# A two-layer decoder trunk in float32: six seven-product pairs per gate/up duo, ScalarE and VectorE in an order set by clocks, and some low parts made by DMA

## The chip, the cores and the metric

The kernel runs on one core of one Trainium2 chip. The metric is the device time of one execution in microseconds (us), lower is better. The profile and the times below are of the kernel before the change.

## The reference

Two layers over 256 tokens with a model width of 2048. The first mixes tokens by gated linear attention, the second by differential attention over shared keys and values; after each stands a gated feed-forward network (FFN). The change touches the two FFNs.

```python
D_MODEL, SEQ, D_FF = 2048, 256, 5632

def swiglu(h, w_gate_up, w_down):
    gate, up = jnp.split(h @ w_gate_up, 2, axis=-1)
    return (jax.nn.silu(gate) * up) @ w_down

for i in range(2):
    h = rmsnorm(x, pre_mix_g[i])
    mix = gla_mixer(h, ...) if i == 0 else diff_mixer(h, ...)
    x = x + rmsnorm(mix, post_mix_g[i])
    f = swiglu(rmsnorm(x, pre_ffn_g[i]), ffn_w_gate_up[i], ffn_w_down[i])
    x = x + rmsnorm(f, post_ffn_g[i])
```

Everything is float32. The weights of an FFN are a 2048 x 11264 matrix (gate and up) and a 5632 x 2048 matrix (down).

## The kernel before

**Three products for one.** A float32 operand is split into a high part of the type fp32r and a low part, the rest. A product is then three TensorE (PE) matmuls into one PSUM bank: high by high, high by low, low by high (`triple`, L442 to L444; for whole chunks L370 to L372). The tokens stand in two blocks of 128, and a matmul has 128 x 128 of tokens as the stationary side and 128 x 512 of weights as the moving one.

**The stream of weights.** `weight_stream` lists in the order of use every unit of weights that PE takes. A plain unit is a "raw" tile of 128 x 1024: two k-tiles of 128 rows by a chunk of 512 columns. `load` (L259) fetches it on SyncE's queue (SP) into one of five slots (NRAW). `split` casts it on ScalarE (ACT, L294) to `hi` and subtracts on VectorE (DVE, L296) to get `lo`. Pairs of hi and lo have nine slots (NRING). PE `take`s a unit, makes 12 matmuls (two k-tiles, two token blocks, three products) and `free`s it. At each take and free `pump` writes out the conversions for which there is room, and the loads for which a raw slot is done with.

**Duos and fast pairs.** A gate chunk c and the up chunk 11 + c go together as a duo (`gated_duo`, `duo_apart`). A duo has eight pairs of k-tiles s. A pair that isn't listed as fast is two plain units, 24 matmuls. For a fast pair seven products do the work of eight, as in Strassen's scheme: 21 matmuls. It has four kinds of unit. Its two raw tiles r1 and r2 go through four sums on DVE (`sums`, L317), which write over the raw tiles and into one tile `sum` of half the width. Then "a" is r1 itself, "b" and "c" are the summed r2 and r1, all 1024 wide, and "d" is the half tile, 512 wide. So three whole tiles and one half are cast and have their low parts made. The half goes to places in the tile `f_ffn_rest`. The seven products need seven PSUM banks; `acc` has six buffers, `tp` has two, which transposes use as well. FAST_FFN names the fast pairs: 0, 2, 3, 4 and 6 of eight. Chunk 1 has four (FAST_SECOND), and chunk 0 is done plainly (`gated_first`). There are ten duos in an FFN, twenty in all.

**The order of steps.** `ffn_steps` lists the up and down steps of an FFN: up 0, up 1, down of chunks 0 and 1, up 2, and so on. A down step has eight plain units (sixteen for a group of two chunks in two steps), 22 times eight in the two FFNs. After a duo, `early` and `late` put the banks together on DVE (L1126), ACT copies one bank (L1137) and applies silu (L1148), and DVE multiplies by the up part (L1130). `gate_T` transposes the result some ticks later (`defer`, `tick`; a tick is a unit or half of one). `evac` adds the down sums (L1202, L1200).

**What sets the order.** The tile scheduler orders the instructions of each engine by simulated times from the order in which the program writes them, with a conversion written as one piece: the cast and the subtraction together.

Of the kernel before, what the change touches and what calls it, by code (L numbers as in the profile page):

```python
# [11 lines left out]
F32 = mybir.dt.float32  # L12
# [3 lines left out]
ALU = mybir.AluOpType  # L16
# [24 lines left out]
FAST_FFN = (0, 2, 3, 4, 6)  # L41
# [6 lines left out]
NRAW, NRING = 5, 9  # L48
V_BEGIN, V_EVERY, V_Q = 16, 3, 1

# [29 lines left out]

def weight_stream():
# [9 lines left out]
    def duo(c1, c2, fast):  # L91
        for s in range(8):
            if s in fast:
                out.extend(("duo", (c1, c2, s), kind) for kind in ("a", "b", "c", "d"))
            else:
                out.extend((name, (n, s), "plain") for name, n in (c1, c2))
# [35 lines left out]
    ffn(1)  # L132
    return out
# [53 lines left out]
class Trunk:  # L187
    def __init__(self, ctx, tc, t):
# [16 lines left out]
        self.subs = {}  # L205
        self.raws = {}
        self.n_dma = self.n_conv = self.n_take = self.n_free = 0
        self.pool_lo = set()
        self.n_narrow = 0
# [46 lines left out]
    def load(self):  # L256
# [3 lines left out]
        self.raws[self.n_dma] = raw  # L260
        self.n_dma += 1
# [28 lines left out]
    def split(self, src, gp=False):  # L290
        nc = self.nc
        w = src.shape[-1]
        hi, lo = self.places(w)
        nc.scalar.copy(hi, src)  # L294
        eng = nc.gpsimd if gp else nc.vector
        eng.tensor_tensor(out=lo, in0=src, in1=hi.bitcast(F32), op=ALU.subtract)  # L296
        return hi, lo

# [11 lines left out]
    def sums(self):  # L310

        nc = self.nc
        r1, r2 = self.pending
        t2 = self.narrow[0].tile([P, C], F32, tag="sum", name=self.uid("sum"))

        def add(out, in0, in1):
            nc.vector.tensor_tensor(out=out, in0=in0, in1=in1, op=ALU.add)  # L317

        add(r1[:, :C], r1[:, :C], r2[:, :C])
        add(r2[:, :C], r2[:, :C], r2[:, C:])  # L320
        add(t2, r1[:, :C], r2[:, C:])
        add(r1[:, C:], t2, r1[:, C:])
        self.pending = r1, r2, t2

    def convert(self):
        n = self.n_conv
        kind = self.stream[n][2]
        self.n_done += kind in ("plain", "beside", "c", "b")
        if kind == "plain":
            self.subs[n] = self.split(self.raw(), n in self.pool_lo) if n else self.split_halves(self.raw())  # L330
        elif kind == "beside":
            self.subs[n] = self.split_beside(self.raw())
        elif kind == "a":
            self.pending = self.raw(), self.raw()
# [1249 lines left out]
```

## Time and profile before

| | |
|---|---|
| median of 3 runs | 2179.21 us (2178.58 to 2179.89) |
| span of the profiled execution | 2177.2 us |
| PE busy, share of the span | 2162.6 us, 99% |
| DVE busy | 1932.7 us, 89% |
| ACT busy | 1267.2 us, 58% |
| GpSimd (POOL) busy | 35.6 us, 2% |
| DMA engines' mean share, SP's queue | 60.2%, 436.44 MB |
| the FFNs | 372 to 1085 us and 1470 to 2177 us of the span |

A row of the timeline gives the start and length in us, the engine, the line, the operation, output and inputs, and in brackets what it waited for. A row of a group ends with its count, the busy time and the mean ns of one, and the idle time ahead of it with what ended it. PEclk in tenths is the clock that TensorE was granted; 9 is 90% or more. PE's matmuls overlap in the pipeline, so the distance of their starts is their price, not the length of one.

### The profile page before, as it was taken

How to read it: one execution, taken by the hardware profiler on the slowest of the kernel's cores; microseconds unless marked ns; L12 is line 12 of the kernel's file. 1: busy time of each engine (PE TensorE's matmuls, PEld its weight loads, DVE VectorE, ACT ScalarE, POOL GpSimd, SP SyncE). 2: the span in 40 equal slices, each digit the busy share in tenths (PEclk: the TensorE clock that was granted, in tenths of full speed). 3: DMA queues.
4: the chain of work that ended last, by engine and by line, in shares of the span. 5: the costliest groups of instructions: out<-in, count | busy, mean ns of one | idle time of the engine just before them, and what ended most of it. 6: DMA issues, size and time to landing. Idle time of an engine off the chain costs nothing.

```text
span 2177.2 us, 28399 instructions
## 1 busy us (share of the span) xinstructions
PE 2162.6 (99%) x10098; PEld 1798.1 (83%) x10098; DVE 1932.7 (89%) x2646; ACT 1267.2 (58%) x1744; POOL 35.6 (2%) x66
## 2 busy tenths in 40 slices
PE   9999999999999999999999999999999999999998
PEld 8887788888888888888878888888888888888886
DVE  7989988998999999998898567889999999999986
ACT  8656665665655555554676455556566555555553
POOL 1000000000000000000000000000000000000000
PEclk9999999999999999999999999999999999999999
DMA  8545566666655566665757655465656555666664
GB/s 309 169 149 191 177 228 213 213 221 215 228 176 199 194 213 213 194 224 189 243 187 248 186 174 161 151 235 189 231 194 223 182 185 195 209 206 212 212 213 135
DMA packets 123315, 440.09 MB, mean 202 GB/s; under 512 B 13899, under 2 KB 16628, under 8 KB 121380
## 3 DMA queue, kind: packets, MB, share of 16 engines
q1 hardware_dynamic: 121996, 436.44, 60.2%
q10 hardware_dynamic: 1176, 1.84, 0.3%
q8 instruction: 79, 1.29, 0.2%
q14 instruction: 64, 0.52, 0.1%
HBM read 429.82 MB, written 9.97 MB: 202 GB/s over the span
## 4 chain that ended last, share of the span: by engine, by line
PE 96%; DVE 2%; DMA 1%; issue 1%; ACT 1%; POOL 0%; SPq 0%; DVEq 0%; POOLq 0%; ACTq 0%
PE acc L444 13%; PE acc L443 13%; PE acc L442 13%; PE acc L372 10%; PE acc L370 10%; PE acc L371 10%; PE acc L585 8%; PE acc L586 4%; PE tp L443 3%; PE tp L444 3%; PE tp L442 3%; PE tp L606 1%; DVE lo L296 1%; PE acc L1307 0%; PE acc L1346 0%
## 5 line engine op out<-in xcount | busy, mean ns | idle before, releaser
L294 ACT CAST hi<-raw 128x1024 fp32r<-128x1024 f32 x905 | 929.5, 1051 | 656.6 <-DVE raw L317 272.7
L296 DVE TENSOR_TENSOR lo<-raw,hi 128x1024 fp32r<-128x1024 f32 x903 | 1077.6, 1220 | 151.8 <-ACT hi L294 148.9
L370 PE MATMUL acc<-hi,f_ffn_gT 128*128 128x512 f32 x704 | 274.1, 390 | 0.0
L371 PE MATMUL acc<-lo,f_ffn_gT 128*128 128x512 f32 x704 | 274.0, 390 | 0.0
L372 PE MATMUL acc<-hi,f_ffn_gT 128*128 128x512 f32 x704 | 268.9, 389 | 0.0
L444 PE MATMUL acc<-hi,h_ffn 128*128 128x512 f32 x666 | 259.6, 390 | 0.0
L443 PE MATMUL acc<-lo,h_ffn 128*128 128x512 f32 x666 | 259.2, 389 | 0.0
L442 PE MATMUL acc<-hi,h_ffn 128*128 128x512 f32 x666 | 258.4, 390 | 0.0
L372 PEld LDWEIGHTS acc<-hi,f_ffn_gT 128*128 128x128 f32 x704 | 132.2, 188 | 27.3
L370 PEld LDWEIGHTS acc<-hi,f_ffn_gT 128*128 128x128 f32 x704 | 132.2, 188 | 27.2
L371 PEld LDWEIGHTS acc<-lo,f_ffn_gT 128*128 128x128 f32 x704 | 132.2, 188 | 27.0
L444 PEld LDWEIGHTS acc<-hi,h_ffn 128*128 128x128 f32 x666 | 125.0, 188 | 26.5 <-issue 0.6
L443 PEld LDWEIGHTS acc<-lo,h_ffn 128*128 128x128 f32 x666 | 125.1, 188 | 25.9
L442 PEld LDWEIGHTS acc<-hi,h_ffn 128*128 128x128 f32 x666 | 125.0, 188 | 25.9
L585 PE MATMUL acc<-h_q,hi 128*128 128x512 f32 x256 | 92.5, 401 | 0.0
L585 PE MATMUL acc<-h_kv,hi 128*128 128x512 f32 x256 | 90.6, 399 | 0.0
L585 PE MATMUL acc<-h_mix,hi 128*128 128x512 f32 x256 | 90.5, 398 | 0.0
L317 DVE TENSOR_TENSOR raw<-sum,raw 128x512 f32<-128x512 f32 x122 | 84.2, 690 | 3.5
L317 DVE TENSOR_TENSOR raw<-raw 128x512 f32<-128x512 f32 x122 | 84.2, 690 | 3.3
L317 DVE TENSOR_TENSOR raw<-raw,raw 128x512 f32<-128x512 f32 x122 | 83.9, 687 | 2.0
L317 DVE TENSOR_TENSOR sum<-raw,raw 128x512 f32<-128x512 f32 x122 | 83.5, 684 | 0.0
L586 PE MATMUL acc<-h_q,lo 128*128 128x256 f32 x256 | 73.2, 286 | 0.0
(416 smaller groups left out, 3912.4 us busy)
## 6 DMA issues: line engine op xcount, KB each, us to landing
raw<-in_w_gu_dram SPq DMA_DIRECT2D x352, 512.0 KB, 4.4
raw<-in_w_d_dram SPq DMA_DIRECT2D x176, 512.0 KB, 5.2
raw<-in_gla_w_r_dram SPq DMA_DIRECT2D x32, 512.0 KB, 4.4
raw<-in_gla_w_v_dram SPq DMA_DIRECT2D x32, 512.0 KB, 4.0
raw<-in_gla_w_out_dram SPq DMA_DIRECT2D x32, 512.0 KB, 4.5
raw<-in_w_v_dram SPq DMA_DIRECT2D x32, 512.0 KB, 4.7
raw<-in_w_k_dram SPq DMA_DIRECT2D x32, 512.0 KB, 4.0
raw<-in_diff_w_q_dram SPq DMA_DIRECT2D x32, 512.0 KB, 3.5
```

The costliest lines, as they stand in the source:

```text
L294: nc.scalar.copy(hi, src)
L296: eng.tensor_tensor(out=lo, in0=src, in1=hi.bitcast(F32), op=ALU.subtract)
L317: nc.vector.tensor_tensor(out=out, in0=in0, in1=in1, op=ALU.add)
L370: nc.tensor.matmul(ps, ah, rh, start=(kt == 0), stop=False)
L371: nc.tensor.matmul(ps, ah, rl, start=False, stop=False)
L372: nc.tensor.matmul(ps, al, rh, start=False, stop=(kt == 2 * ns - 1))
L442: nc.tensor.matmul(ps, ah, wh, start=first, stop=False)
L443: nc.tensor.matmul(ps, ah, wl, start=False, stop=False)
L444: nc.tensor.matmul(ps, al, wh, start=False, stop=last)
L585: nc.tensor.matmul(ps, lh, aT.both(kt), start=(kt == 0), stop=False)
L586: nc.tensor.matmul(ps[:, SEQ:], ll, aT.hi(kt), start=False, stop=(kt == KT - 1))
L606: nc.tensor.transpose(tp[:, j, :], src[:, j * P : (j + 1) * P], self.ident)
```

## The change

**Sixth fast pair.** FAST_FFN gets pair 5. Chunk 1 keeps its four pairs, so 18 of the 20 duos have one pair more; the program has 54 matmuls fewer that are 512 wide (8686 before, 8632 now). In the FFNs the kinds come in the order a, d, b, c, and the first sum is now written to the half tile, not over r1. Banks 5 and 7 of a duo are the ones in `tp`, not 6 and 7. The half tile has two places in the ring `fp` and two in `f_ffn_rest`, before three in `f_ffn_rest`.

**Order by clocks.** A conversion is taken apart into a cast, the sums and the subtraction, each put with its inputs and a duration into a line for ACT or DVE (`sources`, `open`). The code keeps a clock for PE, ACT, DVE and SP: PE's goes on by 227 ns a matmul, and a line's next piece is written as soon as its start by these clocks isn't later than PE's (`emit`, `until`). From the second step of an FFN up to the one before the last (`by_clock`), ACT and DVE issue in the order written; the scheduler's order stands only elsewhere. Silu and the multiplication of a duo go through a side line that is served first.

**Low parts by DMA.** Of every eight down units the third, fifth and seventh (66 in all) have no subtraction on DVE. ACT writes minus the raw tile into the `lo` tile (L408), and a transfer that GpSimd issues adds the weights to it from HBM once more, this time in full float32 (L409). PE's matmul on `lo` waits for that transfer.

**Smaller moves.** `gate_T` of chunk 0 comes after 2 ticks, before 4; the set-up of the attention (`side`) is deferred by 5 ticks, before 20. With the new order its eight DVE steps (L914 to L938) stand in one lump in the first FFN, ahead of a low part.

```diff
-FAST_FFN = (0, 2, 3, 4, 6)
+FAST_FFN = (0, 2, 3, 4, 5, 6)
...
+LO_BY_DMA = {"w_d0": (2, 4, 6), "w_d1": (2, 4, 6)}
...
+LEFT = 1
+PASS_NS, TURN_NS, HELD_NS = 227, 109, 127
+LOAD_NS, LAND_NS, SUM_LAND_NS = 1600, 2800, 10000
...
+def dve_ns(n):
+    return 70 + 1.04 * n
...
+def act_ns(n):
+    return 90 + 0.84 * n
...
+def kinds(chunk):
+
+    return ("a", "d", "b", "c") if chunk[0].startswith("w_gu") else ("a", "b", "c", "d")
...
-    def split(self, src, gp=False):
-        nc = self.nc
-        w = src.shape[-1]
-        hi, lo = self.places(w)
-        nc.scalar.copy(hi, src)
-        eng = nc.gpsimd if gp else nc.vector
-        eng.tensor_tensor(out=lo, in0=src, in1=hi.bitcast(F32), op=ALU.subtract)
-        return hi, lo
...
+            if kind == "a":
+                add(0, raws, lambda: (third(), r1[:, :C], r2[:, :C]))
+                line = self.queue["dve"]
+                if len(line) > 1 and line[-2][1] == ("lo", n - 1) and self.stream[n - 1][2] == "c":
+                    line[-2], line[-1] = line[-1], line[-2]
+                return r1, raws[:1]
+            if kind == "d":
+                add(1, [t1], lambda: (r2[:, :C], r2[:, :C], r2[:, C:]))
+                add(2, [t1], lambda: (r1[:, :C], t[0], r2[:, C:]))
+                return t, [t1]
+            if kind == "b":
+                add(3, [t3], lambda: (r1[:, C:], r1[:, :C], r1[:, C:]))
+                return r2, [t2]
+            return r1, [t4]
...
+        def negated():
+            hl.extend(self.places(w))
+            nc.scalar.activation(hl[1], src(), AF.Copy, scale=-1.0)
+            nc.gpsimd.dma_start(hl[1], self.t[name][idx], accum_op=ALU.add)
+
+        def cast():
+            if not by_dma:
+                hl.extend(self.places(w))
+            nc.scalar.copy(hl[0], src())
+            self.n_done += by_dma
+
+        def rest():
+            eng.tensor_tensor(out=hl[1], in0=src(), in1=hl[0].bitcast(F32), op=ALU.subtract)
+            self.n_done += kind in ("plain", "c", "b")
...
+        if by_dma:
+            self.queue["act"].append((n, ("lo", n), after, act_ns(w), negated))
+            self.queue["act"].append((n, ("hi", n), after, act_ns(w), cast))
         else:
...
+            self.queue["act"].append((n, ("hi", n), after, act_ns(w), cast))
+            self.queue["dve"].append((n, ("lo", n), [("hi", n)], dve_ns(w), rest))
...
+        start = max([self.clock[eng]] + [self.ends[k] for k in after])
+        if start > now:
+            return False
+        line.popleft()
+        fn()
+        self.clock[eng] = self.freed = start + ns
+        self.ends[key] = start + ns + (SUM_LAND_NS if key[0] == "lo" and eng == "act" else 0)
...
+        with self.tc.manual_schedule(engines={mybir.EngineType.Activation, mybir.EngineType.DVE}):
+            yield
+            self.settle()
+            self.until(self.n_conv - 1)
...
-        self.narrow, self.n_narrow = (fp, 0, 3), 0
+        self.narrow, self.n_narrow = (fp, 2, 2), 0
...
-                    self.defer(20, side)
+                    self.defer(5, side)
...
+        step(0, *plan[0])
+        with self.by_clock():
+            for n in range(1, len(plan) - LEFT):
+                step(n, *plan[n])
+        for n in range(len(plan) - LEFT, len(plan)):
+            step(n, *plan[n])
```

How the order changes is seen in the fourth duo of the first FFN. First DVE at its last fast pair, pair 6, before the change. raw_5715 and raw_5763 are the pair's r1 and r2; the rows begin at its first sum (the row with raw_5715 and raw_5763 in, raw_5715 out) and go to its last low part.

```order
L317 TENSOR_TENSOR raw_5715<-raw_5715,raw_5763 128x512
L317 TENSOR_TENSOR raw_5763<-raw_5763 128x512
L317 TENSOR_TENSOR sum_5822<-raw_5715,raw_5763 128x512
L317 TENSOR_TENSOR raw_5715<-sum_5822,raw_5715 128x512
L296 TENSOR_TENSOR lo_5828<-raw_5763,hi_5827 128x1024
L296 TENSOR_TENSOR f_ffn_rest<-sum_5822,f_ffn_rest 128x512
L296 TENSOR_TENSOR lo_5837<-raw_5715,hi_5836 128x1024
```

The same pair on DVE after the change, with raw_5789 as r1 and raw_5834 as r2; lo_5886 belongs to pair 5.

```order
L341 TENSOR_TENSOR sum_5897<-raw_5789,raw_5834 128x512
L418 TENSOR_TENSOR lo_5886<-raw_5745,hi_5885 128x1024
L418 TENSOR_TENSOR lo_5895<-raw_5789,hi_5894 128x1024
L341 TENSOR_TENSOR raw_5834<-raw_5834 128x512
L341 TENSOR_TENSOR raw_5789<-sum_5897,raw_5834 128x512
L418 TENSOR_TENSOR lo_5903<-sum_5897,hi_5902 128x512
L341 TENSOR_TENSOR raw_5789<-raw_5789 128x512
L418 TENSOR_TENSOR lo_5923<-raw_5834,hi_5922 128x1024
L418 TENSOR_TENSOR lo_5938<-raw_5789,hi_5937 128x1024
```

The four sums stood in one row, each reading what the one before had written; now low parts stand between them.

Next DVE from the pair's last low part (lo_5837) to the end of the duo, the first operation of `early`, before the change. All rows but the last are low parts of plain units: two of pair 7, then down units.

```order
L296 TENSOR_TENSOR lo_5837<-raw_5715,hi_5836 128x1024
L296 TENSOR_TENSOR lo_5857<-raw_5775,hi_5856 128x1024
L296 TENSOR_TENSOR lo_5869<-raw_5792,hi_5868 128x1024
L296 TENSOR_TENSOR lo_5878<-raw_5804,hi_5877 128x1024
L296 TENSOR_TENSOR lo_5896<-raw_5831,hi_5895 128x1024
L296 TENSOR_TENSOR lo_5914<-raw_5840,hi_5913 128x1024
L296 TENSOR_TENSOR lo_5926<-raw_5860,hi_5925 128x1024
L296 TENSOR_TENSOR lo_5938<-raw_5872,hi_5937 128x1024
L1126 TENSOR_TENSOR hs_5965<-acc_5707,sg_5964 128x512
```

The same stretch of DVE after the change, from the pair's last low part (lo_5938) on.

```order
L418 TENSOR_TENSOR lo_5938<-raw_5789,hi_5937 128x1024
L418 TENSOR_TENSOR lo_5947<-raw_5851,hi_5946 128x1024
L418 TENSOR_TENSOR lo_5959<-raw_5889,hi_5958 128x1024
L418 TENSOR_TENSOR lo_5968<-raw_5906,hi_5967 128x1024
L418 TENSOR_TENSOR lo_5989<-raw_5941,hi_5988 128x1024
L1297 TENSOR_TENSOR hs_6005<-tp_5753,sg_6004 128x512
L1297 TENSOR_TENSOR sg_6004<-acc_5731,hs_6005 128x512
```

Seven low parts stood between the pair's last one and the first sum of the banks; now there are four, and DVE is less far ahead of PE when it turns to the banks.

Last ACT at the same place, around its copy of the bank (sg_5964), before the change.

```order
L294 CAST hi_5913<-raw_5840 128x1024
L294 CAST hi_5925<-raw_5860 128x1024
L1137 COPY sg_5964<-acc_5666 128x512
L294 CAST hi_5937<-raw_5872 128x1024
L294 CAST hi_5949<-raw_5881 128x1024
L294 CAST hi_5958<-raw_5899 128x1024
L294 CAST hi_5986<-raw_5917 128x1024
L1148 ACTIVATE sg_5964<-sg_5964,rs_ffn_0_3744 128x512
```

ACT around the same copy (sg_6004) after the change.

```order
L414 CAST hi_5967<-raw_5906 128x1024
L414 CAST hi_5988<-raw_5941 128x1024
L408 ACTIVATE lo_6001<-raw_5953 128x1024
L1303 COPY sg_6004<-acc_5712 128x512
L414 CAST hi_6000<-raw_5953 128x1024
L414 CAST hi_6028<-raw_5962 128x1024
L408 ACTIVATE lo_6036<-raw_5974 128x1024
L1317 ACTIVATE sg_6004<-sg_6004,rs_ffn_0_3744 128x512
L1317 ACTIVATE sg_6004<-sg_6004,rs_ffn_1_3849 128x512
L414 CAST hi_6035<-raw_5974 128x1024
```

The negated copies of the first two low parts by DMA of that down step (lo_6001 and lo_6036) stand on ACT among the casts and the bank's copy; GpSimd issues the transfer into each right after it. PE has 50 matmuls between the end of pair 6 and its first use of lo_6001. The raw tile of lo_6001 is loaded into the slot of raw_5851, which DVE is done with at lo_5947.

207 lines of the change are left out of this document (153 added, 54 removed).

## The prediction

> **What bounds the kernel now.** I read the head of the page first, then the busy time by stretch, then the matrix engine's timeline, and last the waits and groups of the engines that feed it. The head gives one core, 2177.2 us, with TensorE (PE) busy throughout at the full granted clock:
>
> ```profile
> span 2177.2 us, 28399 instructions
> PE 2162.6 (99%) x10098; PEld 1798.1 (83%) x10098; DVE 1932.7 (89%) x2646; ACT 1267.2 (58%) x1744; POOL 35.6 (2%) x66
> PEclk9999999999999999999999999999999999999999
> ```
>
> A busy PE need not be a PE at its pace, so the stretches of the two FFNs and, inside the first, one period of two duos with their sixteen down units come next (columns: us, then busy time and count per engine, clock, DMA share, GB/s):
>
> ```profile
> 372.00:1085.00 713.00, 712.76 (x3205) 589.99 (x3204) 656.96 (x826) 408.11 (x510) 3.12 (x5) 1.00 0.62 207
> 1470.00:2177.00 707.00, 697.87 (x3131) 577.79 (x3131) 645.04 (x810) 391.89 (x481) 3.12 (x5) 1.00 0.60 199
> 575.00:700.00 125.00, 125.00 (x562) 103.68 (x561) 118.58 (x141) 69.73 (x78) 0.00 (x0) 1.00 0.60 202
> ```
>
> In that period VectorE (DVE) is busy 118.58 of 125 us, ScalarE (ACT) 69.73 and PE all of it. The timeline of PE at the end of a duo (the fourth of the first FFN) gives the pace:
>
> ```profile
> 655.33 0.39 PE L442 MATMUL acc<-hi,f_ffn_rest 128*128 128x512 f32 x1
> 655.56 0.39 PE L443 MATMUL acc<-lo,f_ffn_rest 128*128 128x512 f32 x1
> ...
> 660.09 0.39 PE L442 MATMUL acc<-hi,h_ffn 128*128 128x512 f32 x1
> ```
>
> Left out are 19 rows of the same kind, so 21 steps take 4.76 us: 0.2267 us a matmul, without a gap. The check is the period: two duos of five fast pairs (21 matmuls each) and six plain units (12 each), with sixteen down units (12 each), are 546 matmuls, 123.8 us, and 16 transposes take the rest of 125. So in the FFNs the number of matmuls is the time, as long as the low parts come ahead of PE. DVE, which makes them, has only some 5% to spare.
>
> **The matmuls.** Eighteen of the twenty duos get a sixth fast pair (chunk 1 of each FFN keeps four). A fast pair is 21 matmuls where two plain units are 24. That removes 18 x 3 = 54 matmuls, 54 x 0.2267 = 12.2 us, all of it on the path. Nothing else leaves PE.
>
> **DVE's work.** The groups of the same period, 575 to 700 us, for DVE (xcount, then busy us and mean ns):
>
> ```profile
> L296 DVE TENSOR_TENSOR lo<-raw,hi 128x1024 fp32r<-128x1024 f32 x59 | 70.4, 1220 | 4.4 <-ACT hi L294 4.1
> L317 DVE TENSOR_TENSOR raw<-sum,raw 128x512 f32<-128x512 f32 x10 | 6.9, 691 | 0.3
> L296 DVE TENSOR_TENSOR f_ffn_rest<-sum,f_ffn_rest 128x512 fp32r<-128x512 f32 x10 | 6.8, 685 | 0.0
> ```
>
> A fast pair has four sums at 0.69, three whole low parts at 1.22 and one half at 0.69: against two plain units it adds 4 x 0.69 + 0.69 + 1.22 = 4.7 us. In the period that is two more pairs, +9.3 us. Six of its sixteen down units lose their DVE low part, -6 x 1.22 = -7.3 us. The new order sets low parts between sums that need each other, and what that is worth stands in DVE's timeline of the fourth duo's last fast pair (pair 6):
>
> ```profile
> 637.37 4.62 DVE L296 TENSOR_TENSOR lo<-raw,hi 128x1024 fp32r<-128x1024 f32 x4
> 642.03 0.69 DVE L317 TENSOR_TENSOR raw<-raw,raw 128x512 f32<-128x512 f32 x1
> 642.76 0.69 DVE L317 TENSOR_TENSOR raw<-raw 128x512 f32<-128x512 f32 x1
> 643.37 0.68 DVE L317 TENSOR_TENSOR sum<-raw,raw 128x512 f32<-128x512 f32 x1
> 644.09 0.69 DVE L317 TENSOR_TENSOR raw<-sum,raw 128x512 f32<-128x512 f32 x1
> 644.70 1.23 DVE L296 TENSOR_TENSOR lo<-raw,hi 128x1024 fp32r<-128x1024 f32 x1
> 645.85 0.69 DVE L296 TENSOR_TENSOR f_ffn_rest<-sum,f_ffn_rest 128x512 fp32r<-128x512 f32 x1
> 646.45 5.76 DVE L296 TENSOR_TENSOR lo<-raw,hi 128x1024 fp32r<-128x1024 f32 x5
> 653.23 2.48 DVE L296 TENSOR_TENSOR lo<-raw,hi 128x1024 fp32r<-128x1024 f32 x2 [1.02 <-ACT hi L294]
> 656.21 1.23 DVE L296 TENSOR_TENSOR lo<-raw,hi 128x1024 fp32r<-128x1024 f32 x1 [0.50 <-ACT hi L294]
> 657.57 0.69 DVE L1126 TENSOR_TENSOR hs<-acc,sg 128x512 f32<-128x512 f32 x1
> ```
>
> A step that waits for the one before starts 0.72 us after it, one that doesn't 0.61 us: two such waits a pair, 0.2 us. Twelve pairs make -2.4 us. DVE's period is then 118.6 + 9.3 - 7.3 - 2.4 = 118.2 us (120.6 without the last term), against PE's 125 - 1.4 = 123.6. On the average PE stays the bound, and DVE costs nothing.
>
> **The lead inside a duo.** Averages hide where it gets tight. By the program's order the third whole low part of pair 4 is the first of the four at 637.37, done at 638.6, and that of pair 6 the first of the five at 646.45, done at 647.7. PE reaches them here (the second is the row at 655.56 above):
>
> ```profile
> 645.36 0.39 PE L443 MATMUL acc<-lo,f_ffn_fast 128*128 128x512 f32 x1
> ```
>
> So DVE leads by 6.8 us at pair 4 and by 7.9 us at pair 6, the plain pair 5 between them having given time back. A whole low part takes 1.13 us in a row of them (5.76 less 1.22, over four). A fast pair costs DVE 4.42 + 2 x 1.13 = 6.7 us before, 6.5 after, against PE's 4.76. With pair 5 fast, pairs 5 and 6 take 2 x 1.74 from the lead of 6.8: 3.3 us is left at pair 6. The rows of the order give another reading: ahead of the first sum that needs pair 6's banks stand seven whole low parts before and four now. DVE's turn at that sum comes with the end of pair 6 on PE, so four at 1.13, less the last, which may just have begun, leave a lead of 2.3 us at least. I take 3; the lowest lead of a duo shrinks from 7 to 3 us, and no stall comes of it.
>
> **ACT and the DMA.** The negated copy is a second ACT pass of a 1024-wide tile, and a fast pair has three whole casts and one half where two stood:
>
> ```profile
> L294 ACT CAST hi<-raw 128x1024 fp32r<-128x1024 f32 x58 | 59.7, 1051 | 49.2 <-DVE raw L317 26.0 <-PE acc L444 6.8 <-DMA raw<-in_w_d_dram 5.8
> L294 ACT CAST f_ffn_rest<-sum 128x512 fp32r<-128x512 f32 x10 | 6.1, 614 | 3.3 <-DVE sum L317 3.3
> ```
>
> Per period: 69.7 + 6 x 1.05 + 2 x 1.67 = 79.4 us of 123.6. ACT has room. The transfers:
>
> ```profile
> q1 hardware_dynamic: 121996, 436.44, 60.2%
> raw<-in_w_gu_dram SPq DMA_DIRECT2D x352, 512.0 KB, 4.4
> raw<-in_w_d_dram SPq DMA_DIRECT2D x176, 512.0 KB, 5.2
> ```
>
> A packet takes 0.602 x 16 x 2177.2 / 121996 = 0.172 us, so a load of 128 packets holds the sixteen engines for 1.4 us. Six more in a period add 8.3 us if they cost the same, 16.5 if they cost double for adding: a share of 0.60 becomes 0.67 to 0.73. The loads on SP keep their order. The new transfers go out on POOL, which has nothing else in the FFNs but the final square roots, and these stand behind the last transfer.
>
> No accumulating transfer is in this trace, so its landing is bounded: 5.2 us if it is like a plain load, twice that, 10.4, if the destination's way counts in full. I take 5.2 + 1.4 = 6.6, nearer to the row. How much time has it? PE's order has 50 matmuls, 11.3 us, between the end of pair 6 and the first such low part. Its raw tile can be loaded only when DVE is done with the first plain unit of pair 7, one low part after pair 6's third; PE uses that third 0.7 us before the end of pair 6, so at a lead of 3 us the load starts 2.6 us before that end, lands at +2.6 and is negated by +3.7. That leaves 7.6 us. If the lead is near 5, it is 9.6. The middle, 8.6, is more than 6.6: no stall. The second and third have four units or more beyond that.
>
> **Once only.** In the first FFN the set-up for the attention (eight DVE steps and two loads, rows before spread over a duo) stands in DVE's order as one lump ahead of a low part. It can cost from nothing to one load's landing, 4.4 us; four down units lie ahead of that low part on PE, so I take 0.5. The borders of the clocked part I price by the largest PE wait in the page of waits, and take nothing:
>
> ```profile
> PEld acc L372 <- DVE h_ffn L647: 2.9, 4, 0.8
> ```
>
> **The sum.** 2177.2 - 12.2 + 0.5 = 2165.5 us of span. The span stands 2.0 below the median of the runs (2179.21), so 2167.5 us.
>
> **Rivals.** *The lead gives out.* DVE waits for ACT 4.1 us in the period, two a duo, when free to take another tile; in a fixed order it may wait more. A lead of 3 is used up by 3.4 us of waits with 0.4 over, 18 x 0.4 = 7 us: 2174.7. From 0.7 over, the gain is gone. For it: 95% load and five fast pairs in a row. Against it: the new order casts each tile a step or more before DVE's turn. Chance 0.18.
>
> *Low parts by DMA land late; this is the slower one.* Place: the third of every eight down units, 22 times. Each us beyond 8.6 costs 22 us; at 9.2 the gain is gone, at 10.4 the time is 2167.5 + 22 x 1.8 = 2207. For it: in stretches where DVE catches up the loads already crowd (ACT waits for them, 5.8 us in the period). Against: 5.2 us in the nearest row. Chance 0.15. [...]
>
> *POOL takes DVE's port.* If POOL's issue of a transfer stops DVE for as long as POOL's small steps last, six a period cost 4 us and 122 of 123.6 still fit; at the length of its 1024-wide step they cost 14.4 us, DVE needs 132.6, and eleven periods lose 99 us: 2267.
>
> ```profile
> L625 POOL TENSOR_TENSOR st<-st,mhalf 128x1 f32<-128x1 f32 x32 | 20.9, 658 | 2005.2 <-DVE st L621 1988.3 <-DVE st L616 16.7 <-POOL st L625 0.2
> L296 POOL TENSOR_TENSOR lo<-raw,hi 128x1024 fp32r<-128x1024 f32 x2 | 4.8, 2404 | 12.2 <-ACT hi L294 12.2
> ```
>
> It decides from 0.9 us each (5.4 us of spare time over six). Chance 0.09. [...]
>
> **Numbers.** The forecast has 0.58. 0.2% (4.4 us) is about what a measurement of this kernel can tell from no change. Faster: 0.58, with 0.12 of the lead's 0.18, 0.04 of the late landing's 0.15 and 0.04 of the port's 0.09: 0.78. Same: 0.04 + 0.03 + 0.02 = 0.09. Slower: 0.02 + 0.08 + 0.03 = 0.13. The range begins at 2165, the sum without the 0.5 and with PE's borders 2 us better. It ends at 2178, which takes in most of the lead's case (0.6 over in every duo) and the lump's upper end, and leaves out some 0.13 of the slower cases and a little below.
>
> **What would show it.** Right: PE's rows 0.2267 us apart through both FFNs, 54 matmuls fewer, the new transfers landing in under 8 us, DVE busy 95 to 97% there. Wrong: PE idle at the low part of the third down unit (late landing), PE idle at pairs 5 and 6 with DVE waiting for ACT (lead), or DVE's low parts longer than 1.22 us beside POOL (port).

## The result and the profile after

The changed kernel takes 2272.12 us (median of 4 runs, 2270.26 to 2279.14), the kernel before 2179.14 (4 runs, 2178.58 to 2179.89): a ratio of 1.043, 95% interval 1.0415 to 1.0446. It is 93 us slower where 12 us faster was forecast.

The head of its page: the span is 91.3 us longer, PE has 54 instructions fewer and is busy 96% where it was 99%.

```profile
span 2268.5 us, 28595 instructions
PE 2187.1 (96%) x10044; PEld 1789.0 (79%) x10044; DVE 1927.4 (85%) x2700; ACT 1361.2 (60%) x1848; POOL 96.2 (4%) x132
PEclk9999999999999999999999999999999999999999
```

Busy time by stretch: the two FFNs, and one period of two duos and sixteen down units, 125 us before and 133.8 now.

```profile
372.00:1128.00 756.00, 724.66 (x3176) 586.23 (x3174) 653.98 (x854) 455.60 (x557) 33.92 (x38) 0.99 0.69 220
1520.00:2268.00 748.00, 706.81 (x3101) 569.29 (x3099) 640.79 (x833) 437.56 (x533) 31.94 (x38) 0.99 0.67 211
612.60:746.40 133.80, 127.25 (x558) 102.20 (x557) 118.68 (x147) 78.50 (x89) 5.29 (x6) 1.00 0.68 213
```

DVE is busy 118.68 us in the period (118.2 was forecast) and ACT 78.50 (79.4): the work is as worked out. The 10 us over the 123.6 that were forecast for the period are idle time on both. Who waits for whom, from the page of waits (us in total, times, longest):

```profile
DVE sum L341 <- DMA raw<-in_w_gu_dram: 58.8, 24, 6.0
PEld acc L603 <- ACT hi L414: 55.0, 65, 1.3
DVE f_ffn_gT L777 <- ACT f_ffn_gT L776: 39.9, 22, 4.5
PEld acc L531 <- DMA lo<-in_w_d_dram: 34.7, 18, 2.5
PE acc L531 <- DMA lo<-in_w_d_dram: 29.2, 18, 2.2
PE acc L603 <- ACT hi L414: 28.8, 54, 0.8
```

L603 is the first of a product's three matmuls in a duo, L531 the second in a down step; PEld (the loading of the stationary side) and PE count much of one wait twice. L777 is DVE's part of the transposes behind a duo, which needs ACT's copy of them (L776). None of these six waits has its like in the page of before. At the end of the fourth duo, where DVE led by 7.9 us before, this is DVE's row with the last two whole low parts of pair 6 (the first two of its four):

```profile
664.13 4.78 DVE L418 TENSOR_TENSOR lo<-raw,hi 128x1024 fp32r<-128x1024 f32 x4
```

And PE's first matmuls on their casts and low parts:

```profile
665.43 0.50 PE L603 MATMUL acc<-hi,h_ffn 128*128 128x512 f32 x1 [0.56 <-ACT hi L414]
666.00 0.39 PE L604 MATMUL acc<-lo,f_ffn_rest 128*128 128x512 f32 x1
...
667.16 0.39 PE L604 MATMUL acc<-lo,h_ffn 128*128 128x512 f32 x1
```

The first low part is done at 664.13 + 1.22 = 665.35 and used at 666.00: DVE's lead, the time by which a low part is ready before PE's first matmul on it, is 0.6 us. At 665.43 PE waits for the cast of the next unit, which ACT could make only after DVE's last sum. Six us later ACT gets the raw tile of the down step's third unit, late, and negates it:

```profile
671.29 1.06 ACT L408 ACTIVATE lo<-raw 128x1024 fp32r<-128x1024 f32 x1 [1.21 <-DMA raw<-in_w_d_dram]
```

GpSimd issues the step's three transfers:

```profile
672.76 0.88 POOL L409 DMA_DIRECT2D lo<-in_w_d_dram  x1 [58.70 <-ACT lo L408]
676.09 0.88 POOL L409 DMA_DIRECT2D lo<-in_w_d_dram  x1 [2.46 <-ACT lo L408]
680.82 0.89 POOL L409 DMA_DIRECT2D lo<-in_w_d_dram  x1 [3.86 <-DVE lo L418]
```

PE comes to the first of these low parts at 679.2 and goes on at 681.0:

```profile
678.94 0.39 PE L530 MATMUL acc<-hi,f_ffn_gT 128*128 128x512 f32 x1
681.01 0.50 PE L531 MATMUL acc<-lo,f_ffn_gT 128*128 128x512 f32 x1 [1.68 <-DMA lo<-in_w_d_dram]
```

Matching each low part's end on DVE with the first matmul that reads it, by the programs' order, gives DVE's lead at the start of a duo, its lowest point and its value at the end, in us, for five duos of the first FFN one after the other (chunks 2 to 6). In the row of before two low parts of each of chunks 2, 4 and 6 are left out, whose first matmuls the scheduler puts ahead of the rest, among those of the down step (their leads are 2.3 to 7.8).

| kernel | at the start | lowest | at the end |
|---|---|---|---|
| before | 16.1, 17.8, 16.3, 17.8, 16.3 | 6.1, 7.1, 6.8, 7.3, 6.8 | 10.7, 10.7, 10.4, 11.0, 10.4 |
| after | 18.9, 7.5, 6.2, 8.3, 7.0 | 3.2, 0.5, 0.3, 0.3, 0.3 | 4.8, 2.1, 2.1, 2.1, 2.1 |

In the first duo with six pairs, pairs 5 and 6 go as forecast: 6.5 us at pair 4, 3.2 at pair 6 (6.8 and 3.3). Its 18.9 is that of the first unit alone, made ahead of the attention's set-up; the third unit, behind it, has 8.6. Then the lead isn't made up for.

Where PE's time went, over both FFNs: the distance from each matmul's start to the next, less the usual one (0.2267 us at 512 columns), put down to the line that came late.

| us | after |
|---|---|
| casts and low parts in the duos | 45.0 |
| low parts by DMA in the down steps | 31.2 |
| matmuls at half clock | 7.4 |
| the rest of the FFNs | 14.3 |
| outside the FFNs, more than before | 7.6 |

That is 105.5; less 1.9 that before lost in its FFNs and 12.2 for 54 matmuls it is 91.4, the whole difference. So the 12.2 us were gained, and 104 lost.

### The profile page after: what moved, and what is told of

The parts are those of the page before. It is cut to its first block, busy times and chain, and to the rows that moved or that the text cites. A ratio compares the mean times of both kernels' runs of the same rounds, so it can differ in the third digit from the quotient of the medians.

```text
span 2268.5 us, 28595 instructions
## 1 busy us (share of the span) xinstructions
PE 2187.1 (96%) x10044; PEld 1789.0 (79%) x10044; DVE 1927.4 (85%) x2700; ACT 1361.2 (60%) x1848; POOL 96.2 (4%) x132
## 3 DMA queue, kind: packets, MB, share of 16 engines
q0 software_dynamic: 9504, 34.61, 8.1%
q10 hardware_dynamic: 1176, 1.84, 0.2%
## 4 chain that ended last, share of the span: by engine, by line
PE 42%; DVE 33%; DMA 13%; issue 7%; ACT 5%; ACTq 0%; POOL 0%; DVEq 0%; SPq 0%; POOLq 0%
DVE lo L418 15%; PE acc L753 8%; DVE raw L341 8%; DMA raw<-in_w_gu_dram 7%; DMA raw<-in_w_d_dram 4%; PE acc L530 4%; PE acc L532 4%; PE acc L531 4%; PE acc L605 4%; PE acc L604 4%; PE acc L603 4%; PE acc L754 4%; ACT hi L414 3%; DVE sum L341 3%; DVE hs L1297 2%
## 5 line engine op out<-in xcount | busy, mean ns | idle before, releaser
L414 ACT CAST hi<-raw 128x1024 fp32r<-128x1024 f32 x923 | 942.4, 1051 | 587.0 <-DVE raw L341 301.5
L418 DVE TENSOR_TENSOR lo<-raw,hi 128x1024 fp32r<-128x1024 f32 x855 | 1023.6, 1221 | 152.6 <-ACT hi L414 148.2
L531 PE MATMUL acc<-lo,f_ffn_gT 128*128 128x512 f32 x704 | 281.0, 400 | 29.2 <-DMA lo<-in_w_d_dram 29.2
L532 PE MATMUL acc<-hi,f_ffn_gT 128*128 128x512 f32 x704 | 275.5, 394 | 0.0
L603 PE MATMUL acc<-hi,h_ffn 128*128 128x512 f32 x612 | 227.5, 396 | 18.4 <-ACT hi L414 18.4
L604 PE MATMUL acc<-lo,h_ffn 128*128 128x512 f32 x612 | 238.4, 390 | 0.0
L605 PE MATMUL acc<-hi,h_ffn 128*128 128x512 f32 x612 | 237.9, 389 | 0.0
L531 PEld LDWEIGHTS acc<-lo,f_ffn_gT 128*128 128x128 f32 x704 | 134.0, 190 | 61.7 <-DMA lo<-in_w_d_dram 34.7
L341 DVE TENSOR_TENSOR raw<-raw 128x512 f32<-128x512 f32 x256 | 175.6, 686 | 0.5
L603 PEld LDWEIGHTS acc<-hi,h_ffn 128*128 128x128 f32 x612 | 114.7, 188 | 56.5 <-ACT hi L414 33.8
L532 PEld LDWEIGHTS acc<-hi,f_ffn_gT 128*128 128x128 f32 x704 | 134.0, 190 | 27.1
L341 DVE TENSOR_TENSOR sum<-raw,raw 128x512 f32<-128x512 f32 x140 | 96.1, 687 | 59.0 <-DMA raw<-in_w_gu_dram 58.8
L605 PEld LDWEIGHTS acc<-hi,h_ffn 128*128 128x128 f32 x612 | 114.9, 188 | 24.0
L409 POOL DMA_DIRECT2D lo<-in_w_d_dram x66 | 58.1, 880 | 1361.8 <-ACT lo L408 699.9
L341 DVE TENSOR_TENSOR raw<-sum,raw 128x512 f32<-128x512 f32 x140 | 96.1, 687 | 0.5
L414 ACT CAST hi<-sum 128x512 fp32r<-128x512 f32 x72 | 44.7, 620 | 63.9 <-DVE sum L341 63.8
```

The lines of the kernel that those rows point to most:

```text
L341: self.nc.vector.tensor_tensor(out=out, in0=in0, in1=in1, op=ALU.add)
L409: nc.gpsimd.dma_start(hl[1], self.t[name][idx], accum_op=ALU.add)
L414: nc.scalar.copy(hl[0], src())
L418: eng.tensor_tensor(out=hl[1], in0=src(), in1=hl[0].bitcast(F32), op=ALU.subtract)
L531: nc.tensor.matmul(ps, ah, rl, start=False, stop=False)
L532: nc.tensor.matmul(ps, al, rh, start=False, stop=(kt == 2 * ns - 1))
```

## The experiments

After the result there were three theories. "Order by clocks" and "scheduler's order" stand for the two ways in which ACT's and DVE's order was set. **D**, the transfers: they fill the DMA engines in the down steps, raw tiles land late, and DVE can't rebuild its lead. **O**, the order: what the clocks hand out keeps DVE close to PE whatever the rest does. **P**, the sixth pair: it takes more of DVE's lead than a down step gives back. The transfers in the page of after, and the DMA share in two windows of 10 us around a down step:

```profile
q0 software_dynamic: 9504, 34.61, 8.1%
raw<-in_w_d_dram SPq DMA_DIRECT2D x176, 512.0 KB, 5.4
lo<-in_w_d_dram POOLq DMA_DIRECT2D x66, 512.0 KB, 8.6
```

```profile
600.00:610.00 10.00, 10.00 (x46) 8.26 (x45) 9.79 (x13) 8.14 (x11) 0.88 (x1) 1.00 0.96 325
610.00:620.00 10.00, 8.80 (x43) 7.08 (x42) 5.10 (x6) 6.19 (x7) 1.78 (x2) 1.00 1.04 269
```

In before, the same place is full for one such window only:

```profile
590.00:600.00 10.00, 10.00 (x46) 8.29 (x45) 8.84 (x10) 6.69 (x8) 0.00 (x0) 1.00 0.96 355
600.00:610.00 10.00, 10.00 (x45) 8.26 (x45) 9.93 (x15) 4.71 (x6) 0.00 (x0) 1.00 0.32 107
```

A packet of the new queue holds an engine for 0.081 x 16 x 2268.5 / 9504 = 0.309 us, where the mean on SP's queue in before is 0.172. A transfer and a load have 144 packets each in the trace of after (128 of 4 KB and 16 of 4 bytes): 2.8 and 1.55 us of all sixteen engines, so a transfer is 1.8 loads. The prediction's 1.4 us for a load counts 128.

### The parts of the change alone

The edits, each on the changed kernel: five pairs, no low parts by DMA, and the scheduler's order.

```diff
-FAST_FFN = (0, 2, 3, 4, 5, 6)
+FAST_FFN = (0, 2, 3, 4, 6)
...
-LO_BY_DMA = {"w_d0": (2, 4, 6), "w_d1": (2, 4, 6)}
+LO_BY_DMA = {}
...
-        with self.tc.manual_schedule(engines={mybir.EngineType.Activation, mybir.EngineType.DVE}):
...
+        yield
```

six_clock_dve: 

> The changed kernel without low parts by DMA: DVE makes all of them. DVE needs 118.2 + 7.3 = 125.5 us per period of two duos where PE needs 123.6. D: DVE is the bound by about 2 us in ten periods, 2165 + 20 = 2185 (2175 to 2200). O or P: PE still waits at the casts and low parts of the duos, and more than after since DVE has more to do, less the late landings: 2230 to 2260.

five_clock_dma: 

> The changed kernel with five fast pairs in a duo (pair 5 plain again). P: the duo takes a fifth less from DVE's lead and PE's waits in the duo go, the late landings stay: 2178 + 22 x 2 = 2222 (2210 to 2230). D: the DMA load is the same, the start lead as well, waits at the end of the duo shrink but stay: 2225 to 2250. O: 2230 to 2260.

six_sched_dma: 

> The changed kernel with the scheduler's order on ACT and DVE: conversions are written as they come and no order is held. O: the lead comes back, only late landings can stay, 2165 to 2210. D: the load stays, and so do most waits: 2240 to 2290. P: 2230 to 2290.

five_clock_dve: 

> The changed kernel with five fast pairs and no low parts by DMA: what is left is the order by clocks, the order of the kinds and the half tile in place of the write over r1. If the order by itself is sound, DVE has 118.6 us less up to 2 in a period of 125: 2175 to 2185. If fixed orders cost time by themselves (a copy for the transposes behind casts that wait, seen at 483 us after), 2190 to 2215.

six_sched_dve: 

> The sixth pair alone: six fast pairs, the scheduler's order, no low parts by DMA. DVE needs 118.6 + 9.3 = 127.9 us in a period of two duos, PE 123.6. In the changed kernel without transfers DVE was busy 95% of the FFNs at 2241. At that share: 127.9 / 0.95 = 134.6, 10 us over the 124.3 of before in ten periods, 2179 + 100 = 2279 less what the first duos' lead covers: 2250 to 2280. If the scheduler's order keeps DVE at 99%: 129.2, 2215 to 2235.

five_sched_dma: 

> The low parts by DMA alone: five fast pairs and the scheduler's order. DVE has 15 us less to do in a period than PE, so only the DMA engines can cost. With the order by clocks the transfers cost 2219.2 - 2187.3 = 32 us at five pairs. If the load delays the raw tiles in any order: 2179 + 32 = 2211, 2195 to 2220. If the clocks' order is what makes it sensitive: 2178 to 2190.

| median us (ratio to before, 95%) | scheduler's order | order by clocks |
|---|---|---|
| five pairs, all on DVE | before | 2187.3 (1.0021 to 1.0047) |
| five pairs, low parts by DMA | 2239.8 (1.0255 to 1.0305) | 2219.2 (1.017 to 1.020) |
| six pairs, all on DVE | 2221.9 (1.0176 to 1.0212) | 2241.4 (1.0267 to 1.0298) |
| six pairs, low parts by DMA | 2281.2 (1.045 to 1.0485) | 2272.1, the change |

(Before stands for the first cell; it differs from it in the order of a pair's kinds and the place of the first sum too, which was not run apart; five_left2 below has them and is level with before.) Within each order the sixth pair and the transfers add up. The sixth pair costs 41 to 43 us in the scheduler's order and 53 to 54 by clocks, the transfers 59 to 61 and 31 to 32. The clocks cost 8 and 20 us without transfers and gain 21 and 9 with them. No part makes the kernel faster, and the transfers, which take work from DVE, make each combination slower. At six pairs without transfers D expected 2185, O and P 2230 to 2260; 2241 speaks for O or P, and the 42 us that the sixth pair costs in the scheduler's order say that six pairs are too many for DVE in either order (P). O's 2165 to 2210 for the scheduler's order with everything else did not come: 2281. With five pairs the waits of the duos were to go and those for late transfers to stay (P, 2222): 2219. P was right on the casts in the duos, but the number is luck: PE's waits for transfers are gone as well. DVE waits for raw tiles longer than in the changed kernel, and PE waits for what DVE then makes late, low parts first:

```profile
DVE sum L341 <- DMA raw<-in_w_gu_dram: 72.1, 18, 5.3
PEld acc L604 <- DVE lo L418: 9.8, 4, 3.1
PEld acc L531 <- DMA lo<-in_w_d_dram: 2.6, 2, 2.3
```

Two runs of the table missed every range that was given: five_sched_dma is 20 us above the higher one, so the transfers cost more in the scheduler's order than by clocks, and five_clock_dve lies between its two.

### What in the transfers costs

six_clock_thin leaves the number, the order and the waits, and takes the bytes away: only 16 of the 1024 columns get the weights added.

```diff
-            nc.gpsimd.dma_start(hl[1], self.t[name][idx], accum_op=ALU.add)
+            nc.gpsimd.dma_start(hl[1][:, :16], self.t[name][idx][:, :16], accum_op=ALU.add)
```

> The changed kernel, but each accumulating transfer adds only 16 of the 1024 columns, so the low parts of the 66 units are wrong outside them: order, waits and the number of transfers are the same, their load on the DMA engines and their landing are not. Theory D (the load: the three transfers of a down step fill the DMA engines, 1.01 to 1.04 there in the profile after, raw tiles land late, and DVE cannot rebuild its lead; PE also waits some 2 us in each of 22 down steps for the first such transfer): both go, 2165 to 2175. Theory O (the order by clocks keeps DVE's lead short whatever the DMA does): only the 22 late landings go, 2272 - 22 x 2 = 2228, 2220 to 2235. Theory P (six fast pairs in a duo take some 10 us from DVE's lead, more than it can gain in a down step): 2220 to 2235 as well.

Measured: 2191.4 us (1.004 to 1.007). 81 of the 93 us are gone, which O and P had not allowed for; D had expected 2165 to 2175, so 16 us or more are left that the bytes don't explain. The wait of DVE for raw tiles falls from 58.8 us to this, and the new queue to a tenth:

```profile
DVE sum L341 <- DMA raw<-in_w_gu_dram: 10.7, 14, 1.7
```

```profile
q0 software_dynamic: 9504, 0.54, 0.8%
lo<-in_w_d_dram POOLq DMA_DIRECT2D x66, 8.0 KB, 5.0
```

six_half_cols adds `[:, :C]`, half of the columns. 

> The changed kernel with each transfer adding 512 of the 1024 columns (the other half of the low part is left wrong): half the bytes. 16 columns gave 2191, all of them 2272. If the DMA engines' load is the cause and is felt only where it fills them, less than half of the 81 us comes back: 2200 to 2230. If the number of transfers or their issue were the cause, 2191 would not have been so near to before, and this run would show 2185 to 2195.

2211.8 (1.0138 to 1.0169): 20 us for the first half of the bytes, 60 for the second; the cost grows faster than the bytes, as it would if it came where the engines fill.

six_later_units gives PE one unit more of time: `(3, 5, 7)` in LO_BY_DMA. 

> The changed kernel with the fourth, sixth and eighth down unit by DMA in place of the third, fifth and seventh. The same load on the DMA engines; the first transfer of a down step has 12 matmuls more, 2.7 us, before PE needs it, and PE waits up to 2.5 us for it after. If the late landing is a cost of its own, PE's 31 us of waits in the down steps go: 2272 - 31 = 2241 (2235 to 2250). If it is only a sign of a missing lead, PE waits as long at the casts and low parts of the duos in place of it: 2262 to 2280.

2276.5 (1.0413 to 1.0472; four runs from 2268.9 to 2282.0, and the profile is of one at 2282.0). PE's waits for transfers fall from 31.2 to 9.1 us, those for casts and low parts in the duos rise from 45.0 to 76.5. With the load there, time gained at the transfer is lost in the duo; the profile is 12 us longer than that of the changed kernel, which is part of the rise.

six_spread takes, of the down units, the seventh only, and the second unit of every plain pair of a duo.

```diff
+LO_BY_DMA = {"w_gu0": (1,), "w_d0": (6,), "w_gu1": (1,), "w_d1": (6,)}
...
+        if kind == "plain" and idx[0] not in ((0, 11) if "gu" in name else ()) and run % 8 in LO_BY_DMA.get(name, ()):
```

> The changed kernel with the same 66 transfers spread out: in each down step the seventh unit alone, and in each duo the second unit of every plain pair. DVE's relief and the bytes are the same. If the transfers hurt because three of them fall into the same 20 us as the thirteen loads that DVE's lead is built from (DMA share 1.01 to 1.04 there after), most of the 81 us between full and 16 columns comes back: 2195 to 2225. If their mean load is what hurts, or a transfer in the duo lands too late where the lead is shortest: 2255 to 2300.

2265.1 (1.0377 to 1.041), only 7 us less, for a reason of its own: PE waits for the transfers inside the duo.

```profile
PEld acc L604 <- DMA lo<-in_w_gu_dram: 41.4, 16, 4.6
...
PE acc L604 <- DMA lo<-in_w_gu_dram: 34.6, 16, 4.2
```

Its waits for casts in the duos are 12.3 us where after had 43.9, so spreading did relieve the loads, but it put the transfers where there is no lead to land in.

six_thin_load was to bring the load back with nobody waiting: beside each small transfer a whole one to a place in HBM.

```diff
+            nc.gpsimd.dma_start(
+                self.dram.tile([P, 1024], F32, tag="dead", name=self.uid("dead"), bufs=4), self.t[name][idx]
+            )
```

> As with 16 columns (2191.4), and beside each of the 66 small transfers a whole one, 128 x 1024 weights from HBM to a place in HBM that nothing reads: the engines' load comes back, nobody waits for it and no low part lands later for its own size. If the load is what delays the raw tiles: 40 to 100% of the 81 us come back, 2223 to 2272. If PE's and DVE's loss came from waiting for the big transfers themselves: 2190 to 2205.

2285.8 (1.0472 to 1.0504), but it tells nothing of the FFNs. The whole transfers depended on nothing in the FFNs, and GpSimd issued the first of them 3.4 us into the program; the loss of 96 us lies before the first FFN, and the FFNs lost 23.8 us where the run with 16 columns lost 18.4. Two runs repair this. In six_thin_load2 the transfers read the fresh tile, which ties them to their place:

```diff
             nc.gpsimd.dma_start(hl[1][:, :16], self.t[name][idx][:, :16], accum_op=ALU.add)
+            for _ in range(2):
+                dead = self.dram.tile([P, 1024], F32, tag="dead", name=self.uid("dead"), bufs=6)
+                nc.gpsimd.dma_start(dead[:, 16:], hl[1][:, 16:].bitcast(F32))
```

> As with 16 columns, and beside each small transfer two of 128 x 1008 from the fresh lo tile to HBM, which nobody waits for at that time: tied to the place in the down step, where the earlier try went out at the start of the program. Engine time as of the whole accumulating transfers, no low part later. If the load is what costs: raw tiles land in up to 11 us as in the changed kernel, and 2235 to 2285. If waiting for the low parts is: 2188 to 2210.

six_thin_twice has the small accumulating line twice, the second waiting for the first. 

> As with 16 columns, each small transfer made twice, the second behind the first: hardly any load on the DMA engines, but a low part is there some 10 us after GpSimd's first issue (two landings of 5.0 us), as late as the 8.6 us of the whole transfers or later. If PE's waiting for late low parts is what costs: 2240 to 2280. If the load is: 2188 to 2205. In between: both have a share, to be read from the waits.

Load alone: 2241.0 (1.0262 to 1.0293), with as much on the new queue as in the changed kernel, and DVE and PE wait as there, for raw tiles and for casts in the duos (L606 here):

```profile
q0 software_dynamic: 20064, 68.68, 8.0%
```

```profile
PEld acc L606 <- ACT hi L417: 64.3, 75, 1.3
DVE sum L341 <- DMA raw<-in_w_gu_dram: 48.8, 19, 5.9
```

Late landing alone: 2238.5 (1.0246 to 1.028). From GpSimd's first issue to the second landing it is 8.9 us in the median, 13.7 at most (8.6 and 11.4 in the changed kernel), and PE waits in the down steps (L532 here):

```profile
PEld acc L532 <- DMA lo<-in_w_d_dram: 54.6, 19, 5.3
PE acc L532 <- DMA lo<-in_w_d_dram: 48.8, 19, 5.0
```

| us over both FFNs | casts, low parts in duos | low parts by DMA | half clock | rest | outside, over before |
|---|---|---|---|---|---|
| after | 45.0 | 31.2 | 7.4 | 14.3 | 7.6 |
| 16 columns | 9.2 | 1.5 | 1.4 | 6.3 | 6.3 |
| and load alone | 52.6 | 2.2 | 0 | 11.6 | 7.9 |
| and late landing alone | 5.9 | 50.8 | 17.2 | 10.5 | -2.6 |

So the transfers cost in two ways, 50 us by the load and 47 by their own landing where each stands alone, and 81 together. How the 81 divide in the changed kernel itself is not shown. Theory D had the first and took the second for a small addition.

### What six pairs would give

five_left2 asks for the 8 us of the clocks at five pairs, whose FFNs lost no more than before's: `LEFT = 2`. 

> Five fast pairs, no low parts by DMA, and the clocked part ends one step earlier: the last two down steps of an FFN are in the scheduler's order, in place of one. With one it was 2187.3, 7.8 over before; PE stood still for 4.1 us at 1087 us of the span, behind the last FFN step of the first FFN, while DVE had low parts ahead of the tokens' transposes, and ran at half clock for 4 us after it. If that border is the whole of it and comes from what DVE has queued at the change of order, it goes: 2178 to 2182. If it comes from the fixed order itself, it stays: 2185 to 2190.

2180.9 (0.9996 to 1.0015): gone. In five_clock_dve this was the row behind the last FFN step of the first FFN:

```profile
1091.69 0.80 PE L532 MATMUL acc<-hi,h_kv 128*128 128x512 f32 x1 [4.09 <-DVE h_kv L818]
```

DVE had five low parts ahead of the transposed tokens that PE waited for. That the order itself does this is not shown: the scheduler's order with six pairs and all on DVE lost 6.8 us more than before outside the FFNs too.

six_thin_left2 and six_thin5_left2 both have 16 columns and LEFT = 2, the second also `(1, 2, 4, 5, 6)` in LO_BY_DMA. 

> As with 16 columns, with the clocked part ended one step earlier, which took 6.5 us away at five pairs: what six pairs would give if the low parts by DMA were nearly free. PE's waits in the FFNs (18.4 us at 16 columns) stay, the border goes: 2191.4 - 6.5 = 2185 (2181 to 2188), so not faster than before even then. If the waits come down with it: 2168 to 2178.

> As the one before, with five of eight down units (the second, third, fifth, sixth and seventh) by transfers of 16 columns in place of three: DVE has another 4 x 1.13 = 4.5 us less in a period. If the sixth pair's 54 matmuls are worth 12.2 us once DVE's lead holds, PE's waits in the FFNs go and the forecast's sum is reached: 2165 to 2171. If something else holds PE at six pairs: over 2178.

2189.6 (1.0028 to 1.0054) and 2190.1 (1.0033 to 1.0063): neither is faster than before, and the first is a little above both its ranges. Outside the FFNs no more than 1.3 us over before is left, but the FFNs lose 23.7 and 26.4, and 4.5 us less work on DVE in a period change nothing. In the same five duos DVE's lead is this, beside two runs shown above:

| kernel | at the start | lowest | at the end |
|---|---|---|---|
| five_clock_dve | 17.3, 11.8, 10.9, 9.8, 10.5 | 6.2, 5.3, 5.2, 3.5, 4.8 | 9.1, 8.0, 7.1, 6.0, 7.4 |
| six_clock_thin | 18.9, 11.5, 9.6, 8.4, 10.5 | 2.6, 1.8, 0.6, 0.3, 1.5 | 4.2, 3.4, 2.2, 2.1, 3.1 |
| six_thin5_left2 | 17.3, 10.8, 10.4, 9.7, 9.3 | 3.2, 1.9, 1.4, 0.5, 0.5 | 4.8, 3.5, 3.0, 2.1, 2.1 |
| six_sched_thin (below) | 16.1, 11.5, 8.9, 10.9, 7.7 | 2.4, 2.6, 0.1, 0.1, 0.1 | 4.2, 4.4, 2.0, 2.0, 2.0 |

By clocks a duo after the first starts with 8 to 12 us where before had 16 to 18, whatever DVE has to do. With five pairs and no transfers 3.5 us or more are left at the lowest point; with six the lead runs out, by clocks and in the scheduler's order alike (the last row, read as that of before). What keeps the start low by clocks, their handing out, the five raw slots or the nine places, is not settled; a sixth slot or a tenth place was not tried.

six_sched_thin: 

> Six pairs, transfers of 16 columns, the scheduler's order. With the whole transfers the scheduler's order was 9 us slower than the clocks' one, with none 19 us faster. If the clocks' order helps where low parts come from elsewhere: 2198 to 2215, slower than the 2191.4 with clocks. If it only costs (border and waits of a fixed order): 2172 to 2188.

2199.8 (1.0079 to 1.0112): without the load the clocks' order is 8 us better than the scheduler's at six pairs. O falls as the main cause.

six_pool lets GpSimd subtract in place of the transfers: the 66 units go into pool_lo, with no time on DVE's clock. 

> The changed kernel with the 66 low parts made by GpSimd (a subtraction of the row of 2.40 us) in place of the transfers: the same relief for DVE, no load on the DMA engines. If GpSimd and DVE work side by side: as with 16 columns, 2185 to 2200. If DVE stands still while GpSimd subtracts, nothing is relieved and 66 x 2.4 = 158 us less the DVE parts saved, 66 x 1.13 = 75, come on top of a DVE that is the bound: 2241 and more, 2240 to 2330.

2247.3 (1.0296 to 1.0326), where it is 2241 with all low parts on DVE: no relief, in the range that was given for a DVE that stands still beside GpSimd. How far it does is not shown; what was measured is that DVE's whole low parts are longer in this run, 3.42 us at most where after has 1.24, and 1.279 us in the mean of 855 where after has 1.221. The first row is DVE's (ns, min/median/max), the second its group, the third GpSimd's:

```profile
L418 DVE TENSOR_TENSOR lo<-raw,hi x855: 1198/1218/3424, 8.5 to 2219.5; 128x1024 fp32r<-128x1024 f32 x171
```

```profile
L418 DVE TENSOR_TENSOR lo<-raw,hi 128x1024 fp32r<-128x1024 f32 x855 | 1072.0, 1279 | 114.9 <-ACT hi L414 110.6
```

```profile
L418 POOL TENSOR_TENSOR lo<-raw,hi 128x1024 fp32r<-128x1024 f32 x68 | 179.5, 2651 | 1237.6 <-ACT hi L414 1004.0 <-PE acc L605 233.6
```

No run was faster than before; five_left2 is level with it.

## Why the prediction was wrong

**The matmuls** were right: 54 fewer, and the account above closes with their 12.2 us. **The work on DVE and ACT** was right: 118.68 and 78.50 us of a period.

**The lead inside a duo** is the step that failed first. It took 6.8 us at pair 4 from a duo of before and subtracted pairs 5 and 6: 3.3. That holds for one duo, the first, with 6.5 and 3.2. For the others a lead as in before was taken as given at the start, and it isn't there: a duo ends with 2 to 5 us where it ended with 10 to 11, and the down step gives back 3 to 6 (6 to 8 with 16 columns, 5 to 7 before). One duo later the lowest is 0.5, and from then on what is missing is PE's time. "On the average PE stays the bound" was true and didn't help: DVE had work for 118 of 124 us, and its waits, 6.4 us of the period before, would have had to shrink; they grew to 15 of 133.8. The rival of the lead had the outcome, a lead that is used up, and half of the cause: that DVE waits more for ACT in a fixed order is so at the copies of the transposes (39.9 us, with nothing like it before), not at the low parts (148.2 us, 148.9 before), and it did not have DVE's waits for raw tiles (58.8). Its 7 us were what is over in single duos, where the sixth pair alone costs 41 to 54.

**ACT and the DMA** failed next. The bound of double time per transfer was right in its number (2.8 us, which is 1.8 loads), and so was the share of 0.67 to 0.73 (0.68). But a share over a period is the wrong row: three transfers, 8.4 us of all engines, come within 8 us, in the burst in which the raw tiles of the down step and the next duo are loaded, and there the share is 1.04. The landing was taken at 6.6 and is 8.6. The 8.6 us that it was given hung on a lead of 3 to 5 us: at 0.6 the raw tile itself comes late. In the rows above the negated copy ended at 672.35, PE came 6.8 us later, and the transfer was there 8.7 us after the copy. The two rivals, priced apart, feed each other: no lead, so late transfers; transfers, so late raw tiles and no lead. The rival of the late landing had 1.8 us times 22; the waits are 31.2 us.

**Once only.** The set-up took its upper end from DVE, a wait of 4.5 us in the first FFN, for a matmul of PE and not for a load. PE had no wait in that duo, but the low parts behind the set-up have a lead of 8.6 us where the one ahead of it has 18.5. The borders were priced at nothing; outside the FFNs 7.6 us were lost (6.3 with 16 columns, and 1.3 when the clocked part ended a step earlier).

**POOL's port** was no cause. No run shows a port; what was measured is that a whole low part took 1.220 us before and 1.221 now, with 66 issues of 0.88 us beside them. The 29 that ran during an issue took 1.220 in the mean, 1.226 at most:

```profile
L418 DVE TENSOR_TENSOR lo<-raw,hi 128x1024 fp32r<-128x1024 f32 x855 | 1023.6, 1221 | 152.6 <-ACT hi L414 148.2
```

Beside GpSimd's issues there was no delay; in six_pool, where GpSimd subtracts in steps of 2.65 us, a low part took up to 2.2 us more.

## What to carry to other kernels

A lead is a stock: when a stage takes more from it, ask what gives it back and how fast, over several rounds, and not only whether one round survives. Price transfers in the window in which they fall (a share of 1.04 here), not by their share of the period (0.68), and count both of their prices: the engines that they hold for others (50 us here, alone), and their own landing for whoever waits (47 us, alone). An engine that is busy 95% of a period may be the bound already: here DVE's other 5% were waits, 6.4 us of 125, and they grew to 15 of 133.8.

## What the runs showed of the hardware

- An accumulating transfer from HBM held the engines 1.8 times as long as a load, per packet (0.309 and 0.172 us) and in all (2.8 and 1.55 us for 144 packets), and 8 KB by the same way took 5.0 us to land, 512 KB 8.6.
- Five times in the FFNs of after PE ran at half clock for 3.41 us. Each time began 0.4 to 1.1 us after PE went on from a wait, of 4.28, 1.91, 2.02, 1.83 and 2.21 us. Behind four other waits of 1.84 to 2.12 us its clock stayed at 1.00; what sets them apart is not shown. In the longest, in the first FFN, it stood for 4.28 us for a copy of transposes that lay on ACT behind casts which waited for DVE's sums. First ACT, then PE, then the window behind it, with a clock of 0.50:

```profile
484.07 0.62 ACT L414 CAST hi<-sum 128x512 fp32r<-128x512 f32 x1 [3.54 <-DVE sum L341]
485.94 1.05 ACT L414 CAST hi<-raw 128x1024 fp32r<-128x1024 f32 x1 [1.25 <-DVE raw L341]
486.89 1.07 ACT L776 CAST f_ffn_gT<-tp 128x512 fp32r<-128x512 f32 x2
```

```profile
487.52 0.50 PE L530 MATMUL acc<-hi,f_ffn_gT 128*128 128x512 f32 x1 [4.28 <-ACT f_ffn_gT L776]
```

```profile
488.00:490.00 2.00, 2.00 (x7) 1.52 (x6) 1.93 (x6) 1.26 (x1) 0.00 (x0) 0.50 0.00 0
```

  Matmuls start 0.43 us apart there, from 487.9 to 491.2. Over the FFNs half clock cost 7.4 us, and 17.2 in the run with late landings alone, whose waits were up to 5.3 us.
- In six_thin_load, whose whole transfers waited for nothing, they filled the DMA engines from the start: in the first 100 us the DMA share was 0.97 and PE was busy 54 us, where it was 0.73 and 97 us in the run with 16 columns alone.

```profile
0.00:100.00 100.00, 54.45 (x206) 40.78 (x206) 25.53 (x63) 32.53 (x69) 33.76 (x75) 0.76 0.97 339
```
